# Eight instead of nine chunks of a feed-forward layer on seven products, with the sums of x formed sooner

## The chip, the cores and the metric

The kernel runs on one core of a Trainium2 chip. The metric is the device time of one execution in microseconds (us), as the median of several runs. Beside it there is one profiled execution, which gives the trace: for each engine, when every instruction started and ended, and what it waited for. The engines are PE (TensorE, matrix products), DVE (VectorE), ACT (ScalarE), POOL (GpSimd) and SP (SyncE, which here only issues loads). PEld is the loading of the stationary operand into PE.

## The reference: what is computed

One layer of a network over 256 tokens of width 2048, in float32:

```
x = LN(a*x + 0.5 * swiglu(x, ffn1))          # feed-forward block 1
x = LN(a*x + mixer(x))                       # mLSTM and stick-breaking attention, gated and merged
x = LN(a*x + 0.5 * swiglu(x, ffn2))          # feed-forward block 2
x = x + sigmoid(x @ w_ple_gate) * (p @ w_ple_proj)

swiglu(x, w1, w3, w2) = (silu(x @ w1) * (x @ w3)) @ w2      # 2048 -> 5632 -> 2048
```

Only the two feed-forward blocks are touched here. Each has two matrices of 2048 x 5632 (w1, w3) and one of 5632 x 2048 (w2).

## The kernel before, in words

**Exact products from reduced ones.** Every operand of a matmul is split into a high part (ACT, L1006 for weights, a cast to the reduced format) and the rest (DVE, L1010, a subtraction). A product is then three matmuls (L1057 to L1059): high x high, high x rest, rest x high. A weight tile holds 256 rows by 512 columns, that is 128 partitions x 1024 elements, 512 KB. One tile against 128 tokens is a *unit*: two blocks of 128 rows, three matmuls each, six matmuls of 512 columns.

**Chunks.** The 5632 hidden columns are cut into 11 chunks of 512. A classical chunk c is gate(c), silu(x @ w1), then hidden(c), the product with x @ w3: 16 units each (8 tiles, two halves of the tokens). After that comes down(c), the product with the chunk's 512 rows of w2: 16 units in four groups of 512 columns, each added into `xres` by L494. Before down(c) can start, the two halves of the hidden values must have been turned: four PE transposes (L264), a cast on ACT (L266) and a subtraction on DVE (L272).

**Seven products.** Nine of the eleven chunks do gate and hidden together by a scheme of Strassen's kind: the two halves of the tokens, pairs of row blocks, and w1 beside w3 form 2 x 2 blocks, and seven products take the place of eight (`seven`). There are four quarters of the 2048 rows, so a chunk has 4 x 7 = 28 units in place of 32. The products have numbers: `one`, `five`, `six`, `two`, `four`, and `rest`, which holds 7 and 3 in turn. The price is in the operands:
- products 5, 6, 7 and 3 need sums of blocks of x (`act.forms`). `form_turn` makes them, once a block, for each of four quarters: four operations of DVE (L282 to L285), then two splits (L258, L259);
- products 5 and 6 need sums of weights. A load `t` of w1 is split for product 1; then a DMA issued by POOL adds a tile of w3 to it in place (`grow`, L328), the sum is split for product 5, a second accumulating DMA is issued, and its result is split for product 6;
- products 4 and 7 need sums that DVE makes (`plus`, L333), from tiles loaded as `b21`, `b12` and `b22`;
- product 6 adds to a bank of PSUM that DVE has seeded (L448) with the difference of products 1 and 5, after ACT has copied product 5 out (L454). Later steps are L459, L462, L470 and L481.

**Order.** The order of all units is a list written out by `ffn`. It has a main list (hidden(0), gate(5), the downs, hidden(5)) and a list of the nine chunks made by `chained`, which also lays the next chunk's product 1 between the last products of a chunk; `None` in it is an empty place. `weave` mixes both evenly: after main unit number m it has placed the share m / n of the second list, so an empty place is a stretch in which only main units run. `Sched` holds small tasks (transposes, silu, forming the sums) that are due some microseconds after they are asked for, on a clock of its own that advances by 6 x 0.2161 us a unit; a unit whose operand is not there yet forces the pending tasks out early.

**Loads and splits.** After each unit `splits_due` splits ahead, up to seven tiles, in the order of the list. `loads` issues plain loads on SP in the order in which they will be needed, as long as fewer than 12 loaded tiles are unsplit or still needed, and the pages in use (44 in all, shared by loads, splits and the turned operands) allow it.

Of the kernel before, what the change touches and what calls it, by code (L numbers as in the profile page):

```python
# [24 lines left out]

PAGES = 44
TEMP_BUFS = 6


RAW_FFN, RAW_MIX, RAW_EDGE = 12, 5, 4  # L30
# [3 lines left out]
SKEW = 6  # L34
# [5 lines left out]


DELAY = {
    "after": 14.0, "form": 18.0, "ln_turn": 5.0, "ln_step": 1.7, "h": 8.0, "silu": 6.0, "late": 9.0, "rest": 1.2, "mt": 3.2,
    "sbt": 4.6, "g0": 3.0, "g1": 4.0, "g2": 12.0, "cv0": 1.0, "cv1": 3.5, "cv2": 1.3,
    "m0": 3.0, "m1": 0.6, "m2": 0.6, "m3": 4.6, "m4": 4.6, "s0": 6.6, "s1": 6.7, "s2": 5.0,
}
# [123 lines left out]
def flat(pairs):  # L170
    return [u for p in pairs for u in p]


def skewed(pairs):
    return [p[0] for p in pairs] + [p[1] for p in pairs]
# [3 lines left out]
def kernel(  # L179
# [81 lines left out]
    def transposed(src, act, c, t):  # L261
        ps = misc([P, 4, P])
        for k in range(4):
            nc.tensor.transpose(ps[:, k], src[:, k * P:(k + 1) * P], ident[:])  # L264
        dst = act.get(c, t)
        nc.scalar.copy(dst[:, 0], ps[:])  # L266
        if act.forms:
            if c not in act.whole:
                act.whole[c] = big()
                pages[0] += 1  # L270
            nc.scalar.copy(act.whole[c][:, t * COL:(t + 1) * COL], ps.rearrange("q k s -> q (k s)"))
        nc.vector.tensor_tensor(out=dst[:, 1], in0=ps[:], in1=dst[:, 0], op=ALU.subtract)  # L272
        act.mark(c, t, 4)
        if act.forms and all(act.ready(c, h) for h in range(TT)):
            sched.spawn(form_turn(act, c), DELAY["form"] + 5.0 * c)

    def form_turn(act, c):

        a = [act.whole[c][:, t * COL:(t + 1) * COL] for t in range(TT)]
        s12, s34 = temp(), temp()  # L280
        l, r = slice(0, 2 * P), slice(2 * P, 4 * P)
        nc.vector.tensor_tensor(out=s12[:, l], in0=a[1][:, l], in1=a[1][:, r], op=ALU.subtract)  # L282
        nc.vector.tensor_tensor(out=s12[:, r], in0=s12[:, l], in1=a[0][:, l], op=ALU.subtract)
        nc.vector.tensor_tensor(out=s34[:, l], in0=a[0][:, l], in1=a[1][:, l], op=ALU.subtract)
        nc.vector.scalar_tensor_tensor(out=s34[:, r], in0=a[0][:, r], scalar=-1.0, in1=s12[:, r],  # L285
                                       op0=ALU.mult, op1=ALU.subtract)
        yield 4.0
        pages[0] -= 1
        for h, src in enumerate((s12, s34)):
            dst = act.forms.get(c, h)  # L290
            split_psum(dst[:, 0], dst[:, 1], src.rearrange("q (k s) -> q k s", s=P))
            drop()
            act.forms.mark(c, h, 4)
# [18 lines left out]
    def seven(wa, wb, rows, col0, cols, act, done):  # L312

        n = rows // (4 * P)
        banks = {k: {} for k in "XEBW"}

        def unit(m, i, tile, src, half, sub, bank, first):
            u = Unit(tile, half, banks[bank], src, i, sub, first and i == 0, i == n - 1,
                     lambda ps, t, m=m: done(m, banks))
            u.onto = not first  # L320
            return u

        def quarter(w, i, sub):
            return rows_of(w, (4 * i + sub) * P, col0, cols)

        def grow(raw, src):
            def load():
                nc.gpsimd.dma_start(out=raw.tile[:, :, :cols], in_=src.src, accum_op=ALU.add)  # L328
            return load

        def plus(a, b):
            def make():
                nc.vector.tensor_tensor(out=a.tile[:, :, :cols], in0=a.tile[:, :, :cols], in1=b.tile[:, :, :cols],  # L333
                                        op=ALU.add)
            return make

        one, five, six, two, four, rest = [], [], [], [], [], []
        for i in range(n):
            t, b21 = quarter(wa, i, 0), quarter(wa, i, 2)
            w1, w5, w6 = Weight(t, [t], []), Weight(t, [], []), Weight(t, [], [])  # L340
            w1.then, w5.then = grow(t, quarter(wb, i, 0)), grow(t, quarter(wb, i, 2))
            one.append(unit(1, i, w1, act, 0, 0, "X", True))
            five.append(unit(5, i, w5, act.forms, 0, 0, "E", True))
            six.append(unit(6, i, w6, act.forms, 0, 2, "B", False))
            two.append(unit(2, i, Weight(b21, [b21], []), act, 0, 2, "X", False))
            four.append(unit(4, i, Weight(t, [], [t, b21], plus(t, b21)), act, 1, 2, "E", False))
            b12, b22 = quarter(wb, i, 0), quarter(wb, i, 2)
            rest.append(unit(7, i, Weight(b12, [b12, b22], [b12], plus(b12, b22)), act.forms, 1, 0, "W", False))
            rest.append(unit(3, i, Weight(b22, [], [b22]), act.forms, 1, 2, "B", False))
        return one, five, six, two, four, rest  # L350

    def chained(parts):

        out = list(parts[0][0])
        for j, (_, five, six, two, four, rest) in enumerate(parts):
            ahead = list(parts[j + 1][0]) if j + 1 < len(parts) else []
            n = len(five)
            out += five + [None] * 3 + six + two[:1]
            for i in range(n):
                out += two[i + 1:i + 2] + four[i:i + 1] + (ahead[i - 2:i - 1] if i >= 2 else [])  # L360
            ahead = ahead[n - 2:]
            for i, u in enumerate(rest):
                out += [u] + ahead[i:i + 1]
        return out
# [56 lines left out]
    def ffn(w1, w3, w2, act, norm, skew=True, ahead=()):  # L421
# [9 lines left out]
        def up(c):  # L431
            s = {}

            def gate(ps, t):
                s[t] = temp()
                activate(s[t][:], ps, ACT.Silu)

            def hidden(ps, t):
                nc.vector.tensor_tensor(out=s[t][:], in0=ps, in1=s[t][:], op=ALU.mult)
                sched.spaced(turn(s[t], c, t), DELAY["h"] + 2.0 * t, TURN_GAP)  # L440

            return group(w1, range(0, D, 2 * P), c * COL, COL, act, gate), group(w3, range(0, D, 2 * P), c * COL, COL, act, hidden)
# [46 lines left out]
        def down(*chunks):  # L489
            pairs = []  # L490
            for g in range(D // COL):
                def add(ps, t, g=g):
                    xs = xres[t][:, g * COL:(g + 1) * COL]
                    nc.vector.scalar_tensor_tensor(out=xs, in0=ps, scalar=0.5, in1=xs,  # L494
                                                   op0=ALU.mult, op1=ALU.add)
                    if n - 1 in chunks:
                        norm.chunk(t, g)
                pairs += group(w2, [c * COL + r for c in chunks for r in (0, 2 * P)], g * COL, COL, hT, add)
            return pairs

        gate, hidden = zip(*(up(c) for c in (0, 5)))
        program.extend((skewed(gate[0][:SKEW]) if skew else flat(gate[0][:SKEW])) + flat(gate[0][SKEW:]))
        rest, tail = down(8, 9), down(10)
        main = flat(hidden[0] + gate[1] + down(0) + down(1) + down(2) + down(3) + down(4) + hidden[1] + down(6) + down(5, 7))
        program.extend(main[:8] + weave(main[8:] + flat(rest[:8]), chained([up7(c) for c in (1, 2, 3, 4, 6, 7, 8, 9, 10)])))
        program.append(norm.load)
        program.extend(ahead)
        program.extend(flat(rest[8:]) + flat(tail[:-SKEW]) + skewed(tail[-SKEW:]))
        boundary(True)


# [446 lines left out]
    def mixing():  # L958
        j = pos["split"]
        return any(-EDGE <= j - e < EDGE for e, _ in edges) or [m for e, m in edges if e <= j][-1:] == [True]  # L960
# [10 lines left out]

    def loads(most=len(raws)):
        while (pos["load"] < most and pos["raw"] < (4 if pos["at"] < 6 else limits(pos["split"])[0])
               and (mixing() or pages[0] + pos["raw"] + 2 * limits(pos["split"])[1] < PAGES)):
            j = pos["load"]
            r = raws[j]
            r.tile = page_pool.tile([P, 2, COL], F32, name="raw", tag="page")
            for ks in pieces(j):
                nc.sync.dma_start(out=r.tile[:, ks, :r.cols], in_=r.src[:, ks])
                if j == 0 and ks.start == 0:  # L980
                    load_x(0, 1)
            if r.plus is not None:
                nc.gpsimd.dma_start(out=r.tile[:, :, :r.cols], in_=r.plus, accum_op=ALU.add)
            pos["load"] += 1
            pos["raw"] += 1
# [111 lines left out]
```

## Time and profile before

| | |
|---|---|
| median of 3 runs | 2329.43 us (2327.81 to 2337.3) |
| profiled execution | 2336.99 us |
| its span, first to last instruction | 2335.2 us |
| mean granted PE clock | 0.979 |
| PE busy | 2229.2 us (95%), 10017 matmuls and transposes |
| DVE busy | 1730.4 us (74%) |
| ACT busy | 1259.3 us (54%) |
| POOL busy | 223.3 us (10%), with 144 accumulating DMAs |

A busy PE is not PE at its peak: matmuls overlap and their ends are modelled, so the distance from start to start tells more than the busy share. In rows of waits "A <- B: 52.8, 12, 6.6" means that A's engine stood idle before A until B was done, 52.8 us in total over 12 times, 6.6 at most. In the timeline a row is start, length, engine, line, operation, what is written and read, and in brackets the idle time before it with what ended it. L numbers are lines of the kernel before.

### The profile page before, as it was taken

Reading aid. Unit: us, or ns where it says so; the run is one execution under the profiler, and the core shown is the slowest. Engines: PE = TensorE matmul, PEld = TensorE weight load, DVE = VectorE, ACT = ScalarE, POOL = GpSimd, SP = SyncE. Lnnn points to the kernel's source line nnn. Section 1 sums busy time; section 2 is a strip of 40 time slices with the busy share of each in tenths; the row PEclk is TensorE's granted clock in tenths of the full one; section 3 lists DMA queues with packets and bytes.
Section 4 is the critical chain, followed back from the end, with each engine's and each line's share of the span. In section 5 each row is a group of like instructions: output and inputs, shape, how many; then the busy total and the mean of one; then the engine's idle time right before and its main releaser. Section 6 shows DMA issues by size and latency. Waiting matters only on the chain.

```text
span 2335.2 us, 27582 instructions
## 1 busy us (share of the span) xinstructions
PE 2229.2 (95%) x10017; PEld 1833.4 (79%) x10017; DVE 1730.4 (74%) x1884; ACT 1259.3 (54%) x1471; POOL 223.3 (10%) x191
## 2 busy tenths in 40 slices
PE   9899999999899999999999999999899999988999
PEld 7677877887777788888888888777787787777878
DVE  6888898897787765654445456888788889778883
ACT  6655565664564455544643453556556566555552
POOL 3111111111000000100100000311110111100000
PEclk9999999999999999999999999999999999999999
DMA  9778988989795565565566577578897798978643
GB/s 325 213 219 244 283 241 224 263 222 278 220 284 183 172 190 160 174 185 157 163 189 191 178 237 234 158 208 234 238 284 224 228 263 232 269 219 263 240 148 104
DMA packets 267208, 510.21 MB, mean 218 GB/s; under 512 B 16000, under 2 KB 25024, under 8 KB 267072
## 3 DMA queue, kind: packets, MB, share of 16 engines
q1 hardware_dynamic: 227904, 432.95, 56.3%
q0 software_dynamic: 39168, 75.51, 18.0%
q8 instruction: 78, 1.28, 0.2%
q14 instruction: 58, 0.48, 0.1%
HBM read 506.30 MB, written 2.10 MB: 218 GB/s over the span
## 4 chain that ended last, share of the span: by engine, by line
PE 52%; issue 15%; DMA 6%; DVE 3%; POOL 2%; ACT 0%; POOLq 0%; ACTq 0%; DVEq 0%
PE mm L1057 15%; PE mm L1059 15%; PE mm L1058 15%; DMA raw<-in_ffn_w_dram 5%; POOL raw L328 2%; PE seeded L1057 2%; PE seeded L1058 2%; PE seeded L1059 1%; PE ms L264 1%; DVE split L1010 1%; DVE xres L403 1%; DMA temp<-in_conv_m_dram 0%; DVE xres L401 0%; DVE xres L404 0%; ACT split L1006 0%
## 5 line engine op out<-in xcount | busy, mean ns | idle before, releaser
L1010 DVE TENSOR_TENSOR split<-raw,split 128x1024 fp32r<-128x1024 f32 (+1 forms) x1037 | 1212.6, 1204 | 350.7 <-ACT split L1006 329.0
L1006 ACT CAST split<-raw 128x1024 fp32r<-128x1024 f32 (+1 forms) x1037 | 1038.1, 1037 | 619.1 <-DMA raw<-in_ffn_w_dram 164.9
L1057 PE MATMUL mm<-split,actT 128*128 128x512 f32 (+2 forms) x2704 | 1059.0, 392 | 18.5 <-ACT actT L258 12.8
L1059 PE MATMUL mm<-split,actT 128*128 128x512 f32 (+2 forms) x2704 | 1049.0, 388 | 12.3 <-DVE actT L272 11.5
L1058 PE MATMUL mm<-split,actT 128*128 128x512 f32 (+2 forms) x2704 | 1047.5, 387 | 5.5 <-DVE split L1010 5.4
L1057 PEld LDWEIGHTS mm<-split,actT 128*128 128x128 f32 x2704 | 513.1, 190 | 121.2 <-ACT actT L258 14.5
L1059 PEld LDWEIGHTS mm<-split,actT 128*128 128x128 f32 x2704 | 512.4, 190 | 121.8 <-DVE actT L272 16.9
L1058 PEld LDWEIGHTS mm<-split,actT 128*128 128x128 f32 x2704 | 513.2, 190 | 106.8 <-DVE split L1010 8.3
L328 POOL DMA_DIRECT2D raw<-in_ffn_w_dram x144 | 175.2, 1228 | 1079.3 <-DVE split L1010 822.3
L1057 PE MATMUL seeded<-split,actT 128*128 128x512 f32 x432 | 177.7, 411 | 52.8 <-DVE seeded L448 52.8
L333 DVE TENSOR_TENSOR raw<-raw 128x1024 f32<-128x1024 f32 x144 | 175.4, 1218 | 54.8 <-DMA raw<-in_ffn_w_dram 54.8
L1058 PE MATMUL seeded<-split,actT 128*128 128x512 f32 x432 | 175.3, 406 | 4.7 <-DVE split L1010 4.7
L1059 PE MATMUL seeded<-split,actT 128*128 128x512 f32 x432 | 173.9, 403 | 0.0
L1057 PEld LDWEIGHTS seeded<-split,actT 128*128 128x128 f32 x432 | 85.0, 197 | 75.2 <-DVE seeded L448 57.8
L266 ACT CAST actT<-ms 128x512 fp32r<-128x512 f32 x84 | 49.1, 588 | 105.7 <-PE ms L264 89.3
L1058 PEld LDWEIGHTS seeded<-split,actT 128*128 128x128 f32 x432 | 85.1, 197 | 24.2 <-DVE split L1010 7.3
L494 DVE SCALAR_TENSOR_TENSOR xres<-mm,xres 128x512 f32<-128x512 f32 x144 | 97.9, 683 | 6.5 <-PE mm L1059 6.5
L1059 PEld LDWEIGHTS seeded<-split,actT 128*128 128x128 f32 x432 | 84.8, 196 | 18.3
L272 DVE TENSOR_TENSOR actT<-ms,actT 128x512 fp32r<-128x512 f32 x84 | 57.1, 684 | 25.2 <-ACT actT L266 13.7
L418 POOL TENSOR_SCALAR xres<-xres 128x512 f32<-128x512 f32 x16 | 28.7, 1836 | 320.0 <-DVE xres L401 300.5
L236 ACT ACTIVATE temp<-mm 128x512 f32<-128x512 f32 (+1 forms) x36 | 20.7, 576 | 48.9 <-PE mm L1059 48.9
L236 ACT ACTIVATE big<-mm 128x512 f32<-128x512 f32 x20 | 12.0, 598 | 55.8 <-PE mm L1059 55.8
(124 smaller groups left out, 641.3 us busy)
## 6 DMA issues: line engine op xcount, KB each, us to landing
raw<-in_ffn_w_dram SPq DMA_DIRECT2D x527, 512.0 KB, 7.9
raw<-in_w_in_dram SPq DMA_DIRECT2D x168, 512.0 KB, 3.8
raw<-in_ffn_w_dram POOLq DMA_DIRECT2D x144, 512.0 KB, 9.7
raw<-in_w_out_dram SPq DMA_DIRECT2D x32, 512.0 KB, 5.2
raw<-in_w_ple_gate_dram SPq DMA_DIRECT2D x24, 512.0 KB, 4.7
raw<-in_w_up_m_dram SPq DMA_DIRECT2D x16, 512.0 KB, 3.7
raw<-in_w_up_sb_dram SPq DMA_DIRECT2D x16, 512.0 KB, 4.3
raw<-in_w_ple_gate_dram SPq DMA_DIRECT2D x16, 256.0 KB, 4.5
```

Of the source, the lines that this page charges most:

```text
L236: nc.scalar.activation(out, in_, func, **kw)
L266: nc.scalar.copy(dst[:, 0], ps[:])
L272: nc.vector.tensor_tensor(out=dst[:, 1], in0=ps[:], in1=dst[:, 0], op=ALU.subtract)
L328: nc.gpsimd.dma_start(out=raw.tile[:, :, :cols], in_=src.src, accum_op=ALU.add)
L333: nc.vector.tensor_tensor(out=a.tile[:, :, :cols], in0=a.tile[:, :, :cols], in1=b.tile[:, :, :cols], op=ALU.add)
L418: nc.gpsimd.tensor_scalar(out=xs, in0=xs, scalar1=ALPHA, scalar2=None, op0=ALU.mult)
L494: nc.vector.scalar_tensor_tensor(out=xs, in0=ps, scalar=0.5, in1=xs, op0=ALU.mult, op1=ALU.add)
L1006: nc.scalar.copy(hi[:, ks], r[:, ks])
L1010: nc.vector.tensor_tensor(out=lo[:, ks], in0=r[:, ks], in1=hi[:, ks], op=ALU.subtract)
L1057: nc.tensor.matmul(ps, hi, w[0][:, k, :u.cols], start=first, stop=False, skip_group_check=u.onto)
L1058: nc.tensor.matmul(ps, hi, w[1][:, k, :u.cols], start=False, stop=False, skip_group_check=u.onto)
L1059: nc.tensor.matmul(ps, lo, w[0][:, k, :u.cols], start=False, stop=last, skip_group_check=u.onto)
```

## The change

Chunk 8 is moved from the seven products to the classical form, so chunks 0, 5 and 8 are classical and eight go by seven products. The main list is put in another order: hidden(5) comes after down(1), gate(8) after down(3); down(4) and down(5) share their groups, so do down(7) and down(8), and down(9) stands alone after the weave. The list of chunks gets eight empty places (`FORMED`) between the first chunk's product 1 and its product 5. The sums of x are due 14 us + 3 us for each quarter after their transposes, in place of 18 + 5. The rule for plain loads keeps one page more free (`SPARE`). The two assignments in `seven` are only written on two lines.

```diff
+FORMED = 8
+SPARE = 1
...
-    "after": 14.0, "form": 18.0, "ln_turn": 5.0,
+    "after": 14.0, "form": 14.0, "ln_turn": 5.0,
...
         if act.forms and all(act.ready(c, h) for h in range(TT)):
-            sched.spawn(form_turn(act, c), DELAY["form"] + 5.0 * c)
+            sched.spawn(form_turn(act, c), DELAY["form"] + 3.0 * c)
...
-            w1.then, w5.then = grow(t, quarter(wb, i, 0)), grow(t, quarter(wb, i, 2))
+            w1.then = grow(t, quarter(wb, i, 0))
+            w5.then = grow(t, quarter(wb, i, 2))
...
     def chained(parts):
 
-        out = list(parts[0][0])
+        out = list(parts[0][0]) + [None] * FORMED
...
-        gate, hidden = zip(*(up(c) for c in (0, 5)))
+        gate, hidden = zip(*(up(c) for c in (0, 5, 8)))
         program.extend((skewed(gate[0][:SKEW]) if skew else flat(gate[0][:SKEW])) + flat(gate[0][SKEW:]))
-        rest, tail = down(8, 9), down(10)
-        main = flat(hidden[0] + gate[1] + down(0) + down(1) + down(2) + down(3) + down(4) + hidden[1] + down(6) + down(5, 7))
-        program.extend(main[:8] + weave(main[8:] + flat(rest[:8]), chained([up7(c) for c in (1, 2, 3, 4, 6, 7, 8, 9, 10)])))
+        rest, tail = down(9), down(10)
+        main = flat(hidden[0] + gate[1] + down(0) + down(1) + hidden[1] + down(2) + down(3) + gate[2] + down(4, 5) + hidden[2] + down(6)
+                    + down(7, 8))
+        program.extend(main[:8] + weave(main[8:], chained([up7(c) for c in (1, 2, 3, 4, 6, 7, 9, 10)])))
         program.append(norm.load)
         program.extend(ahead)
-        program.extend(flat(rest[8:]) + flat(tail[:-SKEW]) + skewed(tail[-SKEW:]))
+        program.extend(flat(rest) + flat(tail[:-SKEW]) + skewed(tail[-SKEW:]))
...
-               and (mixing() or pages[0] + pos["raw"] + 2 * limits(pos["split"])[1] < PAGES)):
+               and (mixing() or pages[0] + pos["raw"] + 2 * limits(pos["split"])[1] < PAGES - SPARE)):
```

More of the change, by code (lines that the diff above doesn't have):

```diff
@@ L42 @@
 DELAY = {
-    "after": 14.0, "form": 18.0, "ln_turn": 5.0, "ln_step": 1.7, "h": 8.0, "silu": 6.0, "late": 9.0, "rest": 1.2, "mt": 3.2,
+    "after": 14.0, "form": 14.0, "ln_turn": 5.0, "ln_step": 1.7, "h": 8.0, "silu": 6.0, "late": 9.0, "rest": 1.2, "mt": 3.2,
     "sbt": 4.6, "g0": 3.0, "g1": 4.0, "g2": 12.0, "cv0": 1.0, "cv1": 3.5, "cv2": 1.3,
```

## The prediction

> **What bounds the kernel now.** I read the stages first: the first feed-forward block, the mixer, the second block, the last projection (columns: window, its length, busy time and instructions of PE, PEld, DVE, ACT, POOL, granted clock, DMA share, GB/s).
>
> ```profile
> span 2335.2 us, 27582 instructions
> ...
> 6.94:759.97 753.03, 707.09 (x3072) 576.11 (x3070) 626.01 (x631) 435.25 (x477) 100.12 (x80) 0.97 0.85 246
> 759.97:1469.69 709.72, 705.19 (x3293) 585.67 (x3293) 403.80 (x518) 344.34 (x451) 21.69 (x25) 1.00 0.62 188
> 1469.69:2222.41 752.72, 706.86 (x3075) 576.87 (x3073) 634.01 (x645) 432.18 (x474) 99.13 (x79) 0.97 0.82 234
> ```
>
> The mixer leaves PE no idle time worth naming. The two blocks do not: DVE is at 83%, DMA at 82 to 85%, and the clock drops to 0.97. What a block would take without waits follows from PE's step, read where matmuls run back to back:
>
> ```profile
> 206.99 0.39 PE L1059 MATMUL mm<-split,actT 128*128 128x512 f32 x1
> ...
> 212.43 0.39 PE L1059 MATMUL mm<-split,actT 128*128 128x512 f32 x1
> ```
>
> 24 steps lie between these two starts: 0.2267 us each, so a unit (six matmuls) is 1.36 us. A block has 492 units, 669 us, and its other 120 PE instructions are short transposes: of its 753 us some 70 to 80 are lost. PE's waits say where:
>
> ```profile
> PE seeded L1057 <- DVE seeded L448: 52.8, 12, 6.6
> PE mm L1057 <- ACT actT L258: 12.8, 3, 7.9
> PE mm L1059 <- DVE actT L272: 11.5, 10, 2.7
> PE mm L1057 <- ACT actT L266: 5.7, 4, 2.5
> PE mm L1058 <- DVE split L1010: 5.4, 5, 2.0
> PE seeded L1058 <- DVE split L1010: 4.7, 5, 1.7
> ```
>
> The first row is the largest: in 12 of the 18 chunks on seven products, product 6 waits until L448 has seeded its bank. The timeline of one such place shows why L448 is late.
>
> ```profile
> 202.81 1.20 POOL L328 DMA_DIRECT2D raw<-in_ffn_w_dram  x1 [17.64 <-DVE split L1010]
> 205.08 2.44 POOL L328 DMA_DIRECT2D raw<-in_ffn_w_dram  x2 [1.07 <-DVE split L1010]
> ...
> 208.54 1.20 POOL L328 DMA_DIRECT2D raw<-in_ffn_w_dram  x1 [1.03 <-DVE split L1010]
> ...
> 215.38 1.05 ACT L1006 CAST split<-raw 128x1024 fp32r<-128x1024 f32 x1 [3.86 <-DMA raw<-in_ffn_w_dram]
> ...
> 218.48 1.99 ACT L1006 CAST split<-raw 128x1024 fp32r<-128x1024 f32 x2 [2.05 <-DMA raw<-in_ffn_w_dram]
> ...
> 220.38 0.58 ACT L454 COPY temp<-mm 128x512 f32<-128x512 f32 x1
> ...
> 222.58 0.80 PE L1057 MATMUL seeded<-split,actT 128*128 128x512 f32 x1 [5.21 <-DVE seeded L448]
> ```
>
> Four accumulating DMAs turn product 5's weights into product 6's. ACT must split these, stands at a split until its DMA has landed, and the copy L454, which L448 needs, is queued behind. So the largest loss is the landing of an accumulation, passed on by ACT's order.
>
> ```profile
> DMA to landing us min/median/max: 5.9/9.7/15.5
> ...
> q1 hardware_dynamic: 67510, 130.97, 56.1%
> q0 software_dynamic: 19584, 37.75, 30.8%
> ...
> raw<-in_ffn_w_dram SPq DMA_DIRECT2D x239, 512.0 KB, 8.0
> raw<-in_ffn_w_dram POOLq DMA_DIRECT2D x72, 512.0 KB, 9.8
> ```
>
> The queue shares are those of 40 to 720 us. An accumulation takes 0.308 x 680 / 72 = 2.9 us of all 16 engines; a plain load 0.561 x 680 / 250 (130.97 MB in pieces of 0.524) = 1.5. Four accumulations in a row alone are 11.6 us. After a long wait the clock costs more, and the chunks differ (windows are from one chunk's product 5 to the next one's; the 4 us window follows the wait above):
>
> ```profile
> 222.58:226.58 4.00, 4.00 (x10) 3.19 (x11) 4.00 (x6) 2.36 (x3) 0.00 (x0) 0.52 0.00 0
> ...
> 428.50:497.10 68.60, 68.60 (x312) 56.79 (x312) 61.32 (x61) 43.22 (x47) 9.86 (x9) 1.00 0.92 252
> ...
> 567.10:647.80 80.70, 71.05 (x303) 57.36 (x302) 61.72 (x60) 42.29 (x47) 11.17 (x10) 0.96 0.81 224
> ...
> sum 661.00, PE 619.36 PEld 505.06 DVE 559.90 ACT 389.55 POOL 81.79; mean PE 68.82 PEld 56.12 DVE 62.21 ACT 43.28 POOL 9.09
> ```
>
> (1 - 0.52) x 4 = 1.9 us go to the clock. Both single windows hold 49 units: 1.40 us a unit at best, 1.65 at worst; the nine of the first block, 433 units, 661.0 us.
>
> **The change part by part**, both blocks together.
>
> *Chunk 8 made classical.* 32 units in place of 28: +8 units, +48 x 0.2267 = **+10.9 us** on PE, which sets the end. Away per block: 12 splits on ACT and DVE, 8 sums L333, 8 accumulations (16 plain loads either way), the seeding of a bank and a few copies.
>
> ```profile
> L1010 DVE TENSOR_TENSOR split<-raw,split 128x1024 fp32r<-128x1024 f32 x352 | 418.8, 1219 | 74.2 <-ACT split L1006 60.6 <-PE mm L1059 7.6 <-PE mm L1058 2.7
> L1006 ACT CAST split<-raw 128x1024 fp32r<-128x1024 f32 x355 | 361.9, 1051 | 254.1 <-DMA raw<-in_ffn_w_dram 83.6 <-DVE raw L333 43.7 <-PE mm L1058 37.5
> ...
> L333 DVE TENSOR_TENSOR raw<-raw 128x1024 f32<-128x1024 f32 x72 | 87.7, 1218 | 26.9 <-DMA raw<-in_ffn_w_dram 26.9
> ```
>
> DVE loses 12 x 1.22 + 8 x 1.22 = 24 us a block, ACT 13, the DMA engines 8 x 2.9 = 23. None of the three sets the end by itself (each is under 90%), so this counts only through waits: the ones on a split (5.4 + 4.7) I halve, **-5**, bounds 0 and -10.
>
> *A longer cover for the accumulations.* The weave lays the chunks' units evenly over the main ones. Before it is 279 places (252 units, 27 empty) over 184 main units, 0.66 main units a place; after, 256 places (224 units, 32 empty) over 216, 0.84. From the first unit of product 5 to that of product 6 are 7 places, 4 of them units: 4 + 7 x 0.66 = 8.6 units before, 4 + 7 x 0.84 = 9.9 after, 1.8 us more. Over 12 waits this is 22 us, the bound on one side. The other is all of them with their clock: 12 x (52.8 / 12 + 1.9) = 76. I take **-40**: chunk 3's product 5 now falls beside hidden(5), as chunk 7's did in the window at 428.5, which has no wait (two waits such as the 5.21 with 1.9 of clock, 14); 1.8 us on the other ten, 18; and some clock where a wait becomes short, 8.
>
> The Trainium skill, in "DMA: Bandwidth & Descriptors", section on the anatomy of one DMA on the gpsimd path, speaks against this term: it fits such a DMA as 2.0 us + bytes / 436 GB/s, by which an estimate for 512 KB is 3.2 us. By that, the accumulations would be down long before and the sum would lose its 40 us; the trace's shortest landing is 5.9 us, so I keep to the trace.
>
> *Sums of x sooner, product 5 of the first chunk later.* The second row of waits: chunk 1's product 5 stood for its sums of x.
>
> ```profile
> 66.79 0.80 PE L1057 MATMUL mm<-split,actT 128*128 128x512 f32 x1 [7.87 <-ACT actT L258]
> ...
> 1529.28 0.50 PE L1057 MATMUL mm<-split,actT 128*128 128x512 f32 x1 [4.17 <-ACT actT L258]
> ```
>
> The last sums, of quarter 3 of x, were due 18 + 5 x 3 = 33 us after its transposes, now 14 + 9 = 23, and eight empty places put 8 x 0.84 = 7 main units, 9 us, in front. 19 us more where 8 were short: both waits go, 12.8 + about 3 of clock, **-16**. Moved earlier are, for each quarter, four DVE operations (0.42 us), two casts and two subtractions, some 3.2 us of DVE; they lie beside gate(0), where DVE is not full:
>
> ```profile
> 0.00:50.00 50.00, 46.23 (x218) 38.08 (x219) 32.31 (x40) 32.19 (x44) 17.90 (x18) 1.00 1.00 339
> ...
> 60.06 0.42 DVE L282 TENSOR_TENSOR temp<-big 128x256 f32<-128x256 f32 x1
> ```
>
> If that cover were gone they would cost 4 x 3.2 a block, so the bounds are -16 and +10. Chunk 1's accumulations gain the same 9 us.
>
> *The main list in another order.* Now down(k) comes sooner after chunk k. Place s of the chunks stands after main unit 8 + s x 216 / 256 (8 are ahead of the weave; chunk 1 has 4 + 8 places in front, then each chunk has 31). Chunk 1 ends at place 42, main unit 44, and down(1) starts at 48; chunk 3 ends at place 104, main unit 96, and down(3) starts at **96**; chunk 4 at 122 for 128. Before, the nearest was chunk 4, at 92 for 96, and that place waits (in the rows on L272 and L266 above):
>
> ```profile
> 366.02 0.55 PE L1057 MATMUL mm<-split,actT 128*128 128x512 f32 x1 [1.82 <-ACT actT L266]
> 368.11 0.80 PE L1059 MATMUL mm<-split,actT 128*128 128x512 f32 x1 [1.11 <-DVE actT L272]
> 371.71 0.80 PE L1057 MATMUL mm<-split,actT 128*128 128x512 f32 x1 [0.67 <-ACT actT L266]
> ```
>
> 3.6 us and 2 of clock, about 6, instead of that chunk's wait for a seeded bank, since everything catches up meanwhile. So down(1) costs 6, less the 2 to 3 that it swallows: +3. Down(3) has no distance: the last product must be scaled on DVE (L470, 0.7), transposed (0.6), cast (0.6) and subtracted (0.7) with a split or two queued ahead on DVE (1.2 each), about 5, then clock and the other half of the rows, 8 in all, and swallows some 4: +4. For both blocks **+15**, bounds 0 (all swallowed) and +28. Down(4, 5) stays as it was.
>
> *One page kept free, chunk 5 held longer.* Weights are loaded while pages in use + loaded weights + 14 stay under 44; now under 43, and the two pages of hidden(5) are held over two chunks more. Followed through the planner's rules, a chunk's last weights (b22) were issued 4 to 10 units ahead of their use in most chunks and 1 to 4 in chunk 9; after, 2 to 6 (but for one) in chunks 3, 6 and 9. A landing of 8.0 us is 5.9 units. Late ones stop DVE and then all behind it, L333's idle time above (26.9). Such a chunk costs 80.7 - 73.4 (661.0 / 9) = 7.3. Two more of them a block would be +29, none 0; with 23 us less for the DMA engines to do, I take **+7**.
>
> The sum: 10.9 - 5 - 40 - 16 + 15 + 7 = **-28 us**. The profiled execution took 2336.99 us (span 2335.2), 7.6 over the median of the runs, 2329.43; I take the difference to that median: **2301 us**. In the bounds' sum the ends are far apart (-91 and +56), and are not all reached together.
>
> **The rivals.** *The chunks run clean.* If the relief of DVE, ACT and DMA lets every chunk run as the window at 428.5: 429 units x 1.40 + 8 more units ahead (10.9) = 611.5 for 661, -49.5 a block, **2230**. For it: that window ran at DMA 0.92 and clock 1.00. Against: its loads came far ahead, and down(1), down(3) stand too near.
>
> *The waits only move.* Each unit loses as before: (661 - 8) / 433 = 1.508 x 429 + 10.9 = 658, -3 a block, **2323**. For it: in the trace a longer wait at one place (366) went with a shorter one at the next, so gains may be spent again at down(3).
>
> *Slower: loads too late.* Where b22 is issued under 5.9 units ahead, L333 stops DVE and the chunk runs at 1.65. Three chunks a block (3, 6, 9) in place of one: 162 x 1.65 + 267 x 1.49 (the rest of before, (661 - 80.7 - 8) / 384) + 10.9 = 676, +15 a block, **2358**. It decides as soon as loads land in over 8 us. For it: the window at 567.1 with its DMA share of only 0.81, so loads were issued late there, not slow. Against: a longer weave gives each chunk 54 units in place of 48.5 for the same 16 plain loads and 8 accumulations.
>
> **Chances.** Forecast (about 2288 to 2316) 0.47, clean 0.12, moved 0.26, late loads 0.15. Range 2258 to 2346: it leaves out most of the clean case and the upper part of the slow one. 0.5%, 11.6 us, is about what a measurement of this kernel can tell from no change. Faster than 2317.8: 0.46 + 0.12 + 0.04 = 0.62; within: 0.25; slower: 0.13.
>
> **What would show it.** The row of L258 gone from PE's waits. The seeded row under 25 us, at most 10 times, none for chunk 1 or 3. A new wait on L266 or L272 right after chunk 3, 4 to 7 us, and one after chunk 1. PE's matmuls 48 more; splits 24 fewer, L333 and L328 16 fewer each. If seeded waits stay near 4.4 us each, the cover was not what counted; if L333's wait on DMA grows past 80 us, late loads decide; a clock of 0.99 in both blocks would speak for the clean case.

## The result and the profile after

The changed kernel takes **2297.12 us** (median of 4 runs, 2295.06 to 2298.76) against 2330.69 for the kernel before on the same chip: a ratio of **0.9852, 95% interval 0.9829 to 0.9874**. The forecast was 2301 us. The profiled execution took 2298.76 us, 38.2 less than that of before, as did its span (2335.2 to 2297.0); the medians differ by 33.6, since the profiled execution of before was one of its longest; the granted clock rose from 0.979 to 0.985. Below, lines of the kernel after are named by their own numbers: L1010 and L1014 are the splits, L1061 to L1063 the matmuls, L451 the seeding, L330 `grow`, L335 `plus`, L268 and L274 the cast and subtraction of turned operands, L473 and L484 product steps on DVE, L497 the addition to `xres`.

The stages of after, in the columns used for before:

```profile
7.01:744.60 737.59, 707.18 (x3093) 577.90 (x3093) 600.94 (x609) 421.71 (x462) 89.84 (x72) 0.98 0.84 246
744.60:1454.38 709.78, 706.58 (x3294) 586.76 (x3293) 404.21 (x518) 344.50 (x451) 20.66 (x25) 1.00 0.62 188
1454.38:2184.20 729.82, 703.78 (x3099) 575.75 (x3096) 609.68 (x623) 418.10 (x459) 88.99 (x71) 0.98 0.82 235
```

All of the gain lies in the two feed-forward blocks: 753.03 to 737.59 and 752.72 to 729.82, together -38.3 us. The mixer is where it was (709.72 and 709.78). PE works as long as before while the blocks are shorter, so it is idle time that went. PE's waits in after:

```profile
PE mm L1061 <- ACT actT L268: 16.5, 10, 3.5
PE mm L1063 <- DVE actT L274: 14.4, 11, 2.7
PE ms L266 <- DVE temp L473: 9.8, 2, 5.5
PE ms L266 <- DVE temp L484: 5.3, 2, 2.8
PE seeded L1061 <- DVE seeded L451: 5.0, 5, 1.1
...
PE mm L1061 <- DVE xres L497: 2.1, 2, 1.4
PE mm L1062 <- DVE split L1014: 1.4, 3, 0.6
...
PE seeded L1062 <- DVE split L1014: 0.8, 2, 0.4
```

Read against the rows of before: the seeded bank went from 52.8 us to 5.0, the sums of x (12.8) have no row any more, the splits went from 10.1 (5.4 + 4.7) to 2.2. The waits on turned hidden values grew: L266 and L272 had 17.2 together (5.7 + 11.5), now L268, L274, L473 and L484 have 46.0. The balance is -47.8 - 12.8 - 7.9 + 28.8 + 2.1 = -37.6 us of waits and +10.9 of added units, -26.7. The remaining -11.5 of the span's -38.2 is about what the clock makes of it: (0.985 - 0.979) x 2228 us of busy PE = 13.

The edit did what it says on the other engines. Here are the operations that touch loaded weights (tile `raw`) in the first block, first of before, then of after; columns DVE, ACT, POOL, each with its instructions:

```profile
6.94:759.97 753.03, 529.05 (x451) 384.73 (x378) 87.07 (x72) 0.97 0.85 246
```

```profile
7.01:744.60 737.59, 504.14 (x431) 372.08 (x366) 77.50 (x64) 0.98 0.84 246
```

Per block ACT has 12 splits less, DVE 12 splits and 8 sums (20), POOL 8 accumulations; DVE saves 24.9 us, ACT 12.7.

Where the new waits are, the timeline of after shows at chunk 3, whose last product is followed at once by down(3):

```profile
302.62 0.68 DVE L473 SCALAR_TENSOR_TENSOR temp<-seeded,temp 128x512 f32<-128x512 f32 x1
...
303.36 1.11 PE L266 MATMUL ms<-ident,temp 128*128 128x128 f32 x4 [4.27 <-DVE temp L473]
...
305.16 0.80 PE L1061 MATMUL mm<-split,actT 128*128 128x512 f32 x1 [0.69 <-ACT actT L268]
...
312.51 1.12 PE L266 MATMUL ms<-ident,temp 128*128 128x128 f32 x4 [2.77 <-DVE temp L484]
...
314.30 0.79 PE L1061 MATMUL mm<-split,actT 128*128 128x512 f32 x1 [0.68 <-ACT actT L268]
```

PE needs the transposes next, the transposes need the scaled product L473, and L473 stands on DVE behind splits. That is 4.27 + 0.69 + 2.77 + 0.68 = 8.4 us idle, and each stop is followed by 4 us at half the clock (column before the last two; the third row is the place after chunk 1, with 0.62):

```profile
303.36:307.36 4.00, 3.31 (x9) 2.48 (x10) 1.77 (x2) 0.59 (x1) 1.19 (x1) 0.50 1.10 262
312.51:316.51 4.00, 3.32 (x9) 2.49 (x10) 0.69 (x1) 0.59 (x1) 0.00 (x0) 0.50 0.30 55
...
154.02:158.02 4.00, 2.65 (x7) 1.73 (x8) 4.00 (x7) 1.94 (x2) 0.00 (x0) 0.62 0.68 247
```

Down(3) thus costs 8.4 + 2 x 2.0 = 12.4 us in the first block. In the second PE stands there for 5.48 + 0.69 + 2.57 + 0.67 = 9.4 us, with clocks of 0.50 and 0.62 behind the two stops, some 13 us in all.

**Why the seeded bank is no longer late.** The same place as in the prediction, chunk 3. First where product 5 begins in before (in the order of units), then the accumulating DMAs of after, its product 5, the copy L457 and its product 6:

```profile
204.49 0.39 PE L1057 MATMUL mm<-split,actT 128*128 128x512 f32 x1
```

```profile
218.43 2.44 POOL L330 DMA_DIRECT2D raw<-in_ffn_w_dram  x2 [16.40 <-DVE split L1014]
...
223.21 2.44 POOL L330 DMA_DIRECT2D raw<-in_ffn_w_dram  x2 [2.33 <-DVE split L1014]
...
224.96 0.39 PE L1061 MATMUL mm<-split,actT 128*128 128x512 f32 x1
...
233.32 0.59 ACT L457 COPY temp<-mm 128x512 f32<-128x512 f32 x1 [2.30 <-PE mm L1063]
...
239.03 0.39 PE L1061 MATMUL seeded<-split,actT 128*128 128x512 f32 x1
```

In before, the last of the four DMAs was issued at 208.54, 4.0 us after product 5 began, and PE wanted product 6 at 222.58 - 5.21 = 217.37, 12.9 us after that beginning. In after the last is issued at about 224.4, half a microsecond before product 5 begins, and product 6 begins 14.1 us after it. Of some 5.8 us gained here, the longer cover is 1.2; the other 4.6 come from the DMAs being issued sooner relative to PE. Taken all together they do not land faster (the view of line L330 in after):

```profile
DMA to landing us min/median/max: 6.0/9.6/14.1
```

(5.9, 9.7 and 15.5 before.) Now the copy waits for PE, where before ACT stood for a DMA.

Two things qualify this. The copy stands behind the split of the third of the four (218.48 in before; the fourth is split after the copy, at 221.91). That third DMA was issued 1.7 us after product 5 began in before and 1.8 us ahead of it in after, and it landed 12.2 us after its issue there and 9.7 here, so at this place a quicker landing helps too. And this place is not the rule: over all chunks (product 5's first unit found in each trace by the order of the units) the last of the four is issued 2.7 us (median) after product 5 begins in before and 1.1 in after, and PE wants product 6 12.9 and 14.5 us after that beginning. On the whole, then, the cover and the sooner issue gain about 1.6 us each.

Last, the sums on DVE (busy, mean ns, idle time before and its releaser) and the plain loads, on the page of before and then of after:

```profile
L333 DVE TENSOR_TENSOR raw<-raw 128x1024 f32<-128x1024 f32 x144 | 175.4, 1218 | 54.8 <-DMA raw<-in_ffn_w_dram 54.8
...
raw<-in_ffn_w_dram SPq DMA_DIRECT2D x527, 512.0 KB, 7.9
```

```profile
L335 DVE TENSOR_TENSOR raw<-raw 128x1024 f32<-128x1024 f32 x128 | 156.0, 1219 | 76.7 <-DMA raw<-in_ffn_w_dram 76.7
...
raw<-in_ffn_w_dram SPq DMA_DIRECT2D x527, 512.0 KB, 7.2
```

DVE waits 21.9 us longer for loads than before, although they land no later.

### The profile page after: what moved, and what is told of

Same layout as the page of the kernel before. It is cut to its first block, busy times and chain, and to the rows that moved or that the text cites. A ratio compares the mean times of both kernels' runs of the same rounds, so it can differ in the third digit from the quotient of the medians.

```text
span 2297.0 us, 27486 instructions
## 1 busy us (share of the span) xinstructions
PE 2228.0 (97%) x10065; PEld 1835.2 (80%) x10065; DVE 1681.4 (73%) x1840; ACT 1231.7 (54%) x1441; POOL 201.8 (9%) x175
## 5 line engine op out<-in xcount | busy, mean ns | idle before, releaser
L1014 DVE TENSOR_TENSOR split<-raw,split 128x1024 fp32r<-128x1024 f32 (+1 forms) x1013 | 1180.7, 1203 | 328.3 <-ACT split L1010 318.9
L1010 ACT CAST split<-raw 128x1024 fp32r<-128x1024 f32 (+1 forms) x1013 | 1011.9, 1037 | 547.8 <-PE mm L1062 141.2
L1061 PE MATMUL mm<-split,actT 128*128 128x512 f32 (+2 forms) x2768 | 1084.9, 392 | 19.0 <-ACT actT L268 16.5
L1063 PE MATMUL mm<-split,actT 128*128 128x512 f32 (+2 forms) x2768 | 1074.6, 388 | 14.4 <-DVE actT L274 14.4
L1062 PE MATMUL mm<-split,actT 128*128 128x512 f32 (+2 forms) x2768 | 1071.8, 387 | 1.4 <-DVE split L1014 1.4
L1063 PEld LDWEIGHTS mm<-split,actT 128*128 128x128 f32 x2768 | 524.6, 190 | 126.7 <-DVE actT L274 21.6
L1061 PEld LDWEIGHTS mm<-split,actT 128*128 128x128 f32 x2768 | 525.0, 190 | 125.3 <-ACT actT L268 20.1
L1062 PEld LDWEIGHTS mm<-split,actT 128*128 128x128 f32 x2768 | 525.4, 190 | 103.9 <-DVE split L1014 2.6
L330 POOL DMA_DIRECT2D raw<-in_ffn_w_dram x128 | 156.0, 1230 | 1058.8 <-DVE split L1014 860.1
L335 DVE TENSOR_TENSOR raw<-raw 128x1024 f32<-128x1024 f32 x128 | 156.0, 1219 | 76.7 <-DMA raw<-in_ffn_w_dram 76.7
L1061 PE MATMUL seeded<-split,actT 128*128 128x512 f32 x384 | 151.6, 395 | 5.0 <-DVE seeded L451 5.0
L1062 PE MATMUL seeded<-split,actT 128*128 128x512 f32 x384 | 150.7, 392 | 0.8 <-DVE split L1014 0.8
L1063 PE MATMUL seeded<-split,actT 128*128 128x512 f32 x384 | 150.5, 392 | 0.0
L268 ACT CAST actT<-ms 128x512 fp32r<-128x512 f32 x84 | 49.1, 589 | 134.1 <-PE ms L266 116.9
L497 DVE SCALAR_TENSOR_TENSOR xres<-mm,xres 128x512 f32<-128x512 f32 x144 | 98.0, 683 | 10.3 <-PE mm L1063 10.1
L1061 PEld LDWEIGHTS seeded<-split,actT 128*128 128x128 f32 x384 | 72.8, 190 | 22.1 <-DVE seeded L451 7.1
L1062 PEld LDWEIGHTS seeded<-split,actT 128*128 128x128 f32 x384 | 72.8, 190 | 16.5 <-DVE split L1014 1.6
L1063 PEld LDWEIGHTS seeded<-split,actT 128*128 128x128 f32 x384 | 72.6, 189 | 15.3
L274 DVE TENSOR_TENSOR actT<-ms,actT 128x512 fp32r<-128x512 f32 x84 | 57.2, 685 | 30.8 <-ACT actT L268 19.7
L266 PE MATMUL ms<-ident,temp 128*128 128x128 f32 x176 | 28.9, 290 | 16.5 <-DVE temp L473 9.8
```

Source lines behind the costliest of these rows:

```text
L1010: nc.scalar.copy(hi[:, ks], r[:, ks])
L1014: nc.vector.tensor_tensor(out=lo[:, ks], in0=r[:, ks], in1=hi[:, ks], op=ALU.subtract)
L1061: nc.tensor.matmul(ps, hi, w[0][:, k, :u.cols], start=first, stop=False, skip_group_check=u.onto)
L1062: nc.tensor.matmul(ps, hi, w[1][:, k, :u.cols], start=False, stop=False, skip_group_check=u.onto)
L1063: nc.tensor.matmul(ps, lo, w[0][:, k, :u.cols], start=False, stop=last, skip_group_check=u.onto)
```

## The experiments

Each is timed against the kernel before on its own chip; differences between two experiments are taken between their ratios, in shares of 2331 us. Unless said otherwise a diff is against the kernel before.

**The downs further from their chunks** (against the kernel after: hidden(5) ahead of down(1), gate(8) ahead of down(3), chunk 5 ahead of 4 and 8 ahead of 7 in the shared downs).

```diff
-        main = flat(hidden[0] + gate[1] + down(0) + down(1) + hidden[1] + down(2) + down(3) + gate[2] + down(4, 5) + hidden[2] + down(6)
-                    + down(7, 8))
+        main = flat(hidden[0] + gate[1] + down(0) + hidden[1] + down(1) + down(2) + gate[2] + down(3) + down(5, 4) + hidden[2] + down(6)
+                    + down(8, 7))
```

> The kernel after with its main list in another order: hidden(5) before down(1), gate(8) before down(3), down(5, 4) and down(8, 7) with the older chunk's rows first, so that no down starts less than 9 main units after its last chunk. Same work. Theory 'the downs stand too near': PE's stops around the first units of down(1), down(3) and down(4, 5), some 64 us of the kernel after with the slow clock behind them, go; 2240 to 2260 us. Rival 'the stops let the accumulations catch up': without them the waits for the seeded bank come back at the next chunks (row of PE seeded on L451 from 5 to over 30 us), and the time stays within 12 us of the kernel after, 2285 to 2309.

Measured: **2255.42 us, ratio 0.9654 (0.9632 to 0.9677)**, 0.0198 x 2331 = 46 us better than after. PE's longest waits:

```profile
PE seeded L1061 <- DVE seeded L451: 15.0, 6, 4.9
PE mm L1063 <- DVE actT L274: 9.0, 7, 2.7
PE mm L1061 <- DVE xres L497: 6.0, 2, 3.2
```

The rows of L268, L473 and L484 are gone and L274 fell to 9.0, so 37.0 of the 46.0 us of waits on turned values in the kernel after went with its order (the kernel before had 17.2). Other waits grew by 13.9 in their place (seeded 10.0, L497 3.9); the clock rose to 0.990.

**The same with a shorter cover** (against that kernel: one empty place between products 5 and 6 in place of three).

```diff
-            out += five + [None] * 3 + six + two[:1]
+            out += five + [None] + six + two[:1]
```

> The same order as the run before, but one empty place instead of three between product 5 and product 6, so that 4 + 5 x 0.9 = 8.5 units lie between their first units, as in the kernel before (8.6), in place of 9.9. Same work. Theory 'cover': the waits for the seeded bank come back, over 25 us in that row, and the time is 20 to 45 us above the run with three places. Rival 'relief' (DVE, ACT and the DMA engines have less to do for each unit of PE, so splits and accumulations are issued sooner): the row stays under 12 us and the time within 10 us of that run.

Measured: 2286.8 us, ratio 0.9797 (0.9762 to 0.9833), 33 us worse than with three places. PE's longest wait:

```profile
PE seeded L1061 <- DVE seeded L451: 48.6, 11, 7.7
```

The seeded wait is back at its size of before, so in this kernel the cover is what holds it off.

**The longer cover alone** (six empty places in the kernel before, which give about the cover that after has).

```diff
-            out += five + [None] * 3 + six + two[:1]
+            out += five + [None] * 6 + six + two[:1]
```

> The kernel before with six empty places instead of three between product 5 and product 6: 4 + 10 x 0.6 = 10 units between their first units, as after the change, with all nine chunks on seven products. Same work. Theory 'cover': the row of PE seeded on L448 falls from 52.8 us to under 25 and the time by 20 to 40 us, to 2290 to 2311. Rival 'relief': the row stays over 40 us and the time within 10 us of the kernel before.

Measured: 2334.32 us, ratio 1.0005 (0.9993 to 1.0018): nothing. The row fell as 'cover' had it, the time stayed as 'relief' had it. PE's longest waits:

```profile
PE mm L1057 <- DVE xres L494: 16.6, 2, 8.3
PE seeded L1057 <- DVE seeded L448: 16.5, 5, 4.8
PE mm L1057 <- ACT actT L266: 16.3, 7, 3.9
PE mm L1059 <- DVE actT L272: 12.1, 12, 2.7
...
PE mm L1057 <- DVE actT L272: 10.9, 2, 5.7
```

The seeded wait fell by 36.3 us, and the same time stands in other rows: 16.6 for L494 and 10.9 for L1057 standing for L272, rows that before doesn't have, and 10.6 more for L266 (5.7 before). The longest of these stops in the timeline:

```profile
279.62 1.21 POOL L328 DMA_DIRECT2D raw<-in_ffn_w_dram  x1 [1.37 <-DVE xres L494]
...
293.61 1.04 ACT L1006 CAST split<-raw 128x1024 fp32r<-128x1024 f32 x1 [1.55 <-DMA raw<-in_ffn_w_dram]
...
294.69 1.23 DVE L1010 TENSOR_TENSOR split<-raw,split 128x1024 fp32r<-128x1024 f32 x1 [1.25 <-ACT split L1006]
...
295.83 0.68 DVE L494 SCALAR_TENSOR_TENSOR xres<-mm,xres 128x512 f32<-128x512 f32 x1
...
296.57 0.79 PE L1057 MATMUL mm<-split,actT 128*128 128x512 f32 x1 [8.34 <-DVE xres L494]
```

ACT still stands at the split until the last accumulation has landed, 14.0 us after its issue. DVE's half of that split stands behind ACT, L494 behind it, and PE wants the bank that L494 empties before it gets to product 6. So cover by itself moved the stop to the next thing in the queue.

**The sums of x alone** (dues and the eight empty places in the kernel before).

```diff
-    "after": 14.0, "form": 18.0, "ln_turn": 5.0,
+    "after": 14.0, "form": 14.0, "ln_turn": 5.0,
...
-            sched.spawn(form_turn(act, c), DELAY["form"] + 5.0 * c)
+            sched.spawn(form_turn(act, c), DELAY["form"] + 3.0 * c)
...
-        out = list(parts[0][0])
+        out = list(parts[0][0]) + [None] * 8
```

> The kernel before with the sums of x due at 14 + 3 us and the eight empty places, nothing else. My step: PE's wait on L258 (12.8 us) and some 3 us of slow clock go, 16 us, so 2313; all other rows of PE's waits as before. Rival: what is won there is lost at chunk 1 or 2, because the stop let everything behind it catch up; 2325 to 2335 with the seeded row over 58 us.

Measured: 2340.79 us, ratio 1.003 (1.0018 to 1.0043). The row of L258 went; of PE's waits these grew, but for the first, which stayed near its 52.8:

```profile
PE seeded L1057 <- DVE seeded L448: 47.7, 13, 8.3
PE mm L1057 <- ACT actT L266: 17.3, 8, 4.4
...
PE seeded L1058 <- DVE split L1010: 13.5, 7, 3.6
```

Alone this part is no gain, rather 7 us of loss: more than the rival allowed, and without its seeded row over 58 us. What was won at the sums was lost at the turned values and the splits.

**The second accumulation taken away** (72 of 144 accumulating DMAs).

```diff
-            w1.then, w5.then = grow(t, quarter(wb, i, 0)), grow(t, quarter(wb, i, 2))
+            w1.then = grow(t, quarter(wb, i, 0))
```

> The kernel before without the second accumulation: product 6 takes the same weight sum as product 5, which leaves out 72 of the 144 accumulating DMAs (chunk outputs are then not the layer's). All splits, sums and matmuls stay. Theory 'landing' (ACT stands at the split of product 6's weights until the DMA is down, and DVE, PE's bank and the turned operands wait behind it): the row of PE seeded on L448 falls from 52.8 to under 10 us, PE's other waits do not take its place, 2255 to 2285 us. Rival 'the queues are simply full' (L454 and L448 come late because splits of every kind stand before them): the row stays over 25 us, 2305 or more.

Measured: **2247.44 us, ratio 0.9616 (0.9597 to 0.9634)**, -90 us. Among the waits of all engines, ACT's at a split for a DMA in the kernel before, then the same here and PE's longest:

```profile
ACT split L1006 <- DMA raw<-in_ffn_w_dram: 164.9, 74, 6.2
```

```profile
ACT split L1006 <- DMA raw<-in_ffn_w_dram: 23.9, 17, 4.2
...
PE mm L1059 <- DVE actT L272: 10.6, 10, 2.7
```

The seeded row is gone altogether, and with it most of what ACT stood for. The gain is more than 'landing' forecast, and more than the 76 us that the prediction had as a bound. It need not be the stop at a split alone: the run also takes 72 DMAs off the queues, and does not part the two.

**The first accumulation taken away** (the other 72).

```diff
-            w1.then, w5.then = grow(t, quarter(wb, i, 0)), grow(t, quarter(wb, i, 2))
+            w5.then = grow(t, quarter(wb, i, 2))
```

> The kernel before without the first accumulation (product 5 takes product 1's tile; the second accumulation for product 6 stays, with its place, its order and its 8.6 units of cover). It leaves out 72 accumulating DMAs, 210 us of all 16 engines. Theory 'DMA load': the second accumulations land sooner when the queues are lighter, the row of PE seeded on L448 falls from 52.8 to under 25 us, 2270 to 2300. Rival 'the second one's own length decides' (four in a row, 2.9 us each, whatever else is under way): the row stays over 40 us, 2315 or more.

Measured: 2275.43 us, ratio 0.9743 (0.9712 to 0.9774), -58 us, with the DMAs that hold up product 6 all there. Here are PE's longest wait, the plain loads on the page (count, size, median us to landing), and the landing of the accumulations (the view of line L328):

```profile
PE seeded L1057 <- DVE seeded L448: 25.4, 11, 4.0
```

```profile
raw<-in_ffn_w_dram SPq DMA_DIRECT2D x527, 512.0 KB, 5.5
```

```profile
DMA to landing us min/median/max: 6.0/9.8/15.1
```

The accumulations left in land as late as ever (9.8); the plain loads land in 5.5 us, where the page of before has 7.9 (its row is quoted above), and the seeded wait halves. So fewer accumulations help the others not by faster landing: their issue comes sooner against PE. Over all chunks the last of the four is issued 0.8 us (median) after product 5 begins, where it was 2.7 before. That plain loads bring this about is a reading; the run also takes away ACT's waits for the first sums, and does not part the two. Nor is it the number of DMAs alone that lets plain loads land sooner: without the second accumulations, also 72 less, they took 7.0 us.

**Less for DVE** (72 of 144 sums L333 left out).

```diff
-            four.append(unit(4, i, Weight(t, [], [t, b21], plus(t, b21)), act, 1, 2, "E", False))
+            four.append(unit(4, i, Weight(t, [], [t, b21]), act, 1, 2, "E", False))
```

> The kernel before without the sums for product 4 (half of L333: 72 operations, 88 us of DVE, which is more than the 50 us that the change takes from DVE; product 4 then takes an unsummed tile). DMA traffic stays. Theory 'landing': DVE is not what is late, the time stays within 15 us of the kernel before. Rival 'DVE relief': the time falls by 25 to 60 us, 2270 to 2308, and the seeded row by half.

Measured: 2308.91 us, ratio 0.9879 (0.9851 to 0.9907), -29 us. PE's longest wait:

```profile
PE seeded L1057 <- DVE seeded L448: 43.4, 12, 5.2
```

The seeded wait loses only 9.4 of 52.8: DVE's load isn't the main thing that holds it. But 29 us are more than the 15 that 'landing' allowed, so DVE's load does cost time: the two rows of waits on splits, 10.1 us before, hold 3.8 here, and the clock rose from 0.979 to 0.984.

**Less for DVE and six empty places** (both edits above).

> The kernel before with both single steps that were tried: six empty places in place of three (alone: no change) and half of the sums L333 left out (alone: 24 to 29 us). Theory 'cover pays only where the engines behind it have slack': together more than their sum, 35 to 60 us under the kernel before, 2275 to 2300, the seeded row under 15 and the L494 row under 8. Rival 'they do not touch': the same as without the sums alone, 2303 to 2315.

Measured: 2315.26 us, ratio 0.9921 (0.9892 to 0.9949), no better than without the cover. That slack on DVE is what makes cover pay falls.

**The other order without the spare page** (the main list of the first experiment with `SPARE = 0`; the changed order itself with no spare page was not tried).

> The better order of the main list (2255 us) with SPARE = 0, so that weights may be loaded one page sooner. My step on pages held that weights issued under 6 units ahead cost time: 5 to 15 us less, 2240 to 2250. Rival: a lighter DMA queue lands them in time anyway, within 6 us, 2249 to 2261.

Measured: 2245.73 us, ratio 0.9611 (0.9589 to 0.9634), against 0.9654 (0.9632 to 0.9677): about 10 us less, at the edge of what the two intervals part. DVE's wait for loads at L335, among the waits of all engines:

```profile
DVE raw L335 <- DMA raw<-in_ffn_w_dram: 46.5, 16, 8.1
```

The kernel after has 76.7 there.

**The other order with the old sums of x** (no empty places in front, dues 18 and 5).

> The better order of the main list with the sums of x due as before (18 + 5 us) and without the eight empty places: undoes that part of the change where the other waits are gone. My step of 16 us: 2267 to 2277, with the row on the cast of the sums (L260 here) back at 10 us or more. Rival from the run of that part alone on the kernel before: what is won there is lost behind it, 2250 to 2262.

Measured: 2264.14 us, ratio 0.9697 (0.9665 to 0.9728), 10 us more than with the new ones, again at the edge. PE's longest wait is on the sums once more:

```profile
PE mm L1061 <- ACT actT L260: 10.9, 3, 4.1
```

**The other order with four empty places**, and then **all three together** (that order, four places, no spare page).

```diff
-            out += five + [None] * 3 + six + two[:1]
+            out += five + [None] * 4 + six + two[:1]
```

> The better order with four empty places instead of three between products 5 and 6 (10.7 units in place of 9.9). Theory 'cover': the waits left at chunk 4 (4.7 and 4.9 us, with the slow clock some 14) go, 2241 to 2250. Rival from the run with six places on the kernel before: PE stops at the next thing that waits behind ACT's split (a bank that L497 must free), so the seeded row falls, the L497 row rises and the time stays within 6 us, 2249 to 2261.

> The better order with SPARE = 0 and four empty places, the two single steps of 10 and 5 us put together. If they add, 2235 to 2242; if both remove the same waits, 2243 to 2249.

Measured: four places alone 2250.18 us, ratio 0.9628 (0.9608 to 0.9649), not told apart from three, though the seeded row fell from 15.0 to 5.2 (that of L497 went from 6.0 to 7.7). All three together **2242.11 us, ratio 0.9603 (0.9573 to 0.9633)**: the best seen, 58 us (0.0249 x 2331) better than the kernel after, though not told apart from the one without the spare page. Of its waits on PE, the longest and the seeded one:

```profile
PE mm L1063 <- DVE actT L274: 9.0, 7, 2.7
...
PE seeded L1061 <- DVE seeded L451: 2.7, 2, 1.4
```

## Why the prediction came out right, and where its steps did not

The time was right to 4 us and inside its range, but two terms of the sum were off by 25 to 30 us each, in opposite directions. That the sum came out so close is luck; that the time fell, and at the waits that were named, is not.

- **Eight more units, +10.9.** Right: 10065 matmuls and transposes on PE's page for 10017, in blocks where nothing else was added to PE. The other engines lost the work that was named. The waits on splits, set at -5, lost 7.9.
- **The cover for the accumulations, -40.** Mis-sized, and half wrong in its reason. The seeded waits lost 47.8 us, and by the prediction's own 1.9 us of clock for each long wait, 12 x 1.9 more: some -70 as an estimate, near the bound of -76. That the second accumulation is what ACT and the seeded bank wait for held (without it the row is gone, and 90 us with it and the lighter queues). That 1.8 us of cover would pay for it did not hold as such: in the kernel before the same cover gave nothing. It pays in the other order (33 us for two places). Sooner issue is not what parts the two: over all chunks the last of the four DMAs is issued 1.9 us (median) after product 5 begins, and product 6 is wanted 14.2 to 14.3 us after, in the kernel before with six places and in the other order alike. What differs is what stands next in the queues: L494, L266 and L272 hold 55.9 us of PE's waits in the first (16.6 + 16.3 + 12.1 + 10.9), their counterparts 15.0 in the second (L497 6.0, L274 9.0). What keeps these short, the eight fewer accumulations a block, the thinner share of chunk units in the weave or the places of the downs, wasn't settled. DVE's relief was ruled out as the thing that makes cover pay. What it adds by itself wasn't measured for the change; 88 us less of DVE brought 29 in the kernel before, so the change's 50 us may be worth some 16 by proportion, an estimate, where the prediction had 5 for all relief.
- **The rule on an accumulating DMA.** By the fit that the Trainium skill gives ("DMA: Bandwidth & Descriptors", anatomy of one DMA on the gpsimd path), an estimate of 3.2 us, the term would have been nothing. The traces of these DMAs, which accumulate and have plain loads beside them, disagree: medians of 9.6 after and 9.8 without the first accumulations, never under 6.0, and taking the second ones away moved the end by 90 us.
- **Sums of x sooner, -16.** The wait went, as forecast. Its worth depends on what comes next: nothing in the kernel before (ratio 1.003), where the waits on L266 and on product 6's splits grew by 11.6 and 8.8 us, and about 10 us beside the better order. The weight given to the whole 16 was too much.
- **The main list in another order, +15.** Mis-sized, beyond its bound of +28. The places were right (after chunk 1, worst after chunk 3), and so was the chain of steps at down(3), though PE stood a step earlier in it, at the transposes behind L473. But down(3) cost 12 to 13 us a block and not 8, since both halves of the rows stop PE and each stop is followed by a clock of 0.50 to 0.62; and the part set to be "swallowed" was counted from seeded waits that no longer existed. The waits grew by 28.8 us; with about 2.0 us of clock for each of the four stops at down(3) and (1 - 0.62) x 4 = 1.5 for the two after chunk 1 that is +40 as an estimate. The run with the other order bears it out: 46 us, some 8 of which are waits that the kernel before had too (17.2 against 9.0).
- **The spare page, +7.** Consistent: about 10 us in the other order, and the sums' wait on loads rose to 76.7, just under the 80 named. The rival of late loads is thereby out: plain loads land in 7.2 us at the median, not above 8. (Its own sum, 15 us a block over 2329.43, gives about 2360 and not 2358.)

Of the rivals, "the waits only move" describes both single parts (the longer cover alone and the sums alone) and the way the downs took back the accumulations' gain, but not the whole: 33.6 us stayed. "Clean", 2230 us, was not reached by the change; the best kernel of the runs came within 12 us of it.

## What to carry to other kernels

A consumer's distance in the written order must be counted from the last step of its producer through every queue that step stands in: here the downs near their chunks, down(3) at distance zero and down(1) at four units above all, cost more than the whole change gained (46 us by the run with the other order, against 33.6). Where an engine takes its work in the written order, as ACT and DVE do in these traces, a longer cover for one late thing helps only until the next thing queued behind the same stop, so look there before paying for cover. And when two terms of a sum share waits ("swallowed"), they can't both be counted: with the accumulations' term at what it came to, the downs had next to nothing left to swallow.

## What the runs showed of the hardware

- A short stop of PE can cost some 2 us more in clock: after 2.77 us of idle time the next 4 us, from the four transposes on, had a granted clock of 0.50, after 5.21 us one of 0.52. The Trainium skill ("TensorE: Matmul & The Clock Gate", the part on the clock gate) speaks of an idle window of about 3.4 us; here a stop shorter than that was enough, since the four transposes right behind the 2.77 us already took 1.12 us, where the same four took 0.60 at 233.12.
- An accumulating DMA of 512 KB lands in 9.2 to 10.1 us (the median of a run) whether 144, 128 or 72 of them run. The plain loads beside them go from 7.9 to 5.5 us when the first 72 are taken away, but only to 7.0 when the second 72 are.
